# Operands laid out by numpy before the launch in a one-core hybrid decoder step: kept conv rows, cached keys, taps and sinks turned, states and second weights in whole rows

## The chip, the cores and the metric

The kernel runs on one core of a Trainium2 chip. The time is what the device takes for one execution, in microseconds; several runs are made and their median is taken. What numpy does ahead of the launch and behind it is outside this time.

## The reference

A trunk of two layers works on one prompt of 1024 tokens and on 8 decode rows of 4 tokens each (32 sample tokens), all 1024 wide. Each layer computes `x + gate * Branch(RMSNorm(x) * (1 + scale) + shift)`, and a last RMSNorm follows.

```python
# layer 0: attention, 16 heads of 64 over 4 key heads, window 128, a sink for each head;
# sample tokens also look at 128 cached keys and values of their row
k_all = jnp.concatenate([k_buf, k], axis=1)
p = sink_softmax(einsum('bqkgd,bskd->bkgqs', q, k_all) * SWA_SCALE, mask, sinks)
# layer 1: gated DeltaNet
xqkv, z, a, b = jnp.split(h @ w_in, [4096, 6144, 6160], axis=-1)
xpad = jnp.concatenate([conv_buf, xqkv], axis=1)   # 3 kept rows, then the new ones
conv = silu(depthwise_conv(xpad, conv_w))          # 4 taps on each of 4096 channels
...
o, s_new = gated_delta_chunked(q, k, v, g, beta, s0, chunk)
return o @ w_out, xpad[:, -3:], s_new
```

What the change touches are these inputs and outputs. In: `cache_swa_k` (8 rows x 128 positions x 4 heads x 64), `state_gdn_conv` (8 x 3 x 4096), `state_gdn_s` (8 rows x 16 heads x 128 x 128), `swa_sinks` (16), `gdn_conv_w` (4 x 4096) and `gdn_w_in` (1024 x 6176). Out: the last three conv inputs of the prompt and of each sample row, and the new 128 x 128 states of the prompt (16) and of the sample rows (8 x 16).

## The kernel before

**Layout.** Prompt and samples are one matrix of T = 1056 columns (TP = 1024 for the prompt, TS = 32 for the samples), cut into three column groups of 384, 384 and 288; the samples are the end of the third. A float32 product is made of three matmuls on split halves: high times high, high times low, low times high (`wh`, `wl` for weights, `hhi`, `hlo` and `h2hi`, `h2lo` for activations). A projection of one block of 128 output channels takes, for each group, 8 slices of the contraction by three matmuls; `projector` (L575 to L612) runs a list of such blocks and loads the raw weights two blocks ahead (`load_raw`, L441), which ScalarE rounds to `wh` and GpSimd subtracts to `wl` (`split_w`, L449).

**Stages**, in the times of the profiled execution: 0 to 107 us norm, modulation and the first projections; to 407 attention with its projections; to 560 its output projection and the second modulation; to 1410 the DeltaNet projections, with the conv, the triangular solves and the chain of states woven in; then the last output projection, with the sample rows' states read, updated and written, and the last norm.

**What sets the order.** Up to L1287 the instructions go to the tile framework's own scheduler, with some pinned behind others. From there on class `Core` (L96 to L175) keeps a modelled clock for each engine, and each instruction is kept in program order on its engine; every instruction passes through the helper at L89, so most rows of the profile carry that line. The kernel's parts are generators ("jobs") started by `weave` with a rank from the tables `K` and `KR` (L241, L242). Between projection matmuls the planner advances jobs whose condition holds: `ready` (operands written by now on the modelled clock), `soon` (a little later), `idle` (an engine free about now), or `bank` (one of PSUM's eight tiles free: two `pj` for projections, one `tr`, two `mi`, one `ob`, two `lg`; L232). The tables are the same in both kernels.

**The places that the change touches.**

- Sinks. `hsel`, a constant 128 x 128 selector (L59 to L63), is loaded at L1223 to L1225; 16 sinks are loaded as a column (L1248), and a matmul (L1250) spreads them to 128 partitions, from where VectorE writes them negated to `ssk` (L1251). `ssk` is used in the softmax of the cached pairs.
- Cached keys. `cached_pair` (L1067 to L1133) runs four times, each for two decode rows. It loads keys and values (`kc`, `vc`: position on the partition, 256 channels in a row), and for each row transposes four heads on TensorE (L1083) into one `mi` bank, which ScalarE copies to `KT` (L1085). Logits, softmax, two transposes of the probabilities and the value matmuls follow. `cached` (L1034 to L1063) starts the pairs once the prompt's attention is done, and behind the last pair it frees their tiles, loads the rest of the output weights and calls `begin_out`, which loads the gate's selector rows `selt`.
- Taps. `first_weights` (L1431 to L1445) loads the taps as rows (`cwr`), transposes them on TensorE into an `lg` bank, and VectorE copies them to `cw`; it also loads the first key weights `kwr`.
- Second weights. `gin` (L1313) is `gdn_w_in` seen as 128 partitions x 8 slices x 6176 columns. A raw half block is 128 partitions by 4 slices by 128 columns, so 4 pieces of 512 B for each partition. The decay columns `wab` (L1523) are pieces of 32 columns.
- Conv. `conv` (L1668 to L1730) is called for 32 blocks of 128 channels, at the projection of each. ScalarE's evacuation `evac` writes the projection to one of two tiles `XR` (channels on the partition, 3 + T columns), applies the first tap, and VectorE the others. At the third group the kept rows of the samples are loaded (`st`, 24 rows of 128 channels, L1695), and `samples()` (L1699 to L1726) waits for a `tr` bank, transposes `st` and the last 35 columns of `XR` (3 of the prompt, 32 of the samples) on TensorE, and ScalarE copies the first to `XS` and the second to `cvo`. SP then stores `cvo` in four pieces: the prompt's rows and three for the samples. GpSimd copies the samples' new columns into `XS` and does their four taps; ScalarE applies SiLU and SP stores the result. `open_["st"]` keeps the next block's third group from being evacuated before this job has ended.
- States. `states_times` (L2381 to L2421) loads the sample rows' states in tiles of four heads (`S0`, L2364), and `new_states` (L2631 to L2675) loads them again, updates them and stores them to `S1` (L2365). Each partition's share of a tile is four pieces of 512 B. The prompt's new states are stored two heads at a time (L2104).

Of the kernel before, what the change touches and what calls it, by code (L numbers as in the profile page):

```python
# [5 lines left out]
F32 = mybir.dt.float32  # L6
# [8 lines left out]
P = 128  # L15
D = 1024
KD = D // P
TP = 1024
NB = TP // P
DB = 8  # L20
# [11 lines left out]
def constants():  # L32

    i = np.arange(P)
    blocks = {}
    blocks["ident"] = np.eye(P)
    blocks["iu"] = (i[:, None] <= i[None, :]) * 1.0
    blocks["ones"] = np.ones((P, P))
    blocks["mku"] = np.where(i[:, None] <= i[None, :], 0.0, NEG)
    dist = P + i[:, None] - np.arange(2 * P)[None, :]  # L40
    blocks["wmask"] = np.where((dist >= 0) & (dist <= P), 0.0, NEG)

    t, par = i % DS, i // 16 % 2
# [15 lines left out]
    hsel = np.zeros((P, P))  # L59
    for kv in range(4):  # L60
        for r in range(32):
            hsel[kv * 4 + (r % 16) // 4, 32 * kv + r] = 1.0
    blocks["hsel"] = hsel  # L63
# [4 lines left out]
    order = ["ident", "iu", "ones", "mku", "lo32", "bsel", "fold32", "fold64", "wmask", "hsel", "smask", "selp", "sels"]  # L68
# [151 lines left out]
def body(tc, I, O, cst_ap, dbg=None):  # L220
# [299 lines left out]
    def ready(*ts):  # L520
        return lambda: plain() or nc.ready(ts) <= nc.free["tensor"]
# [4 lines left out]
    def idle(eng, *ts):  # L526
        return lambda: plain() or max(nc.free[eng], nc.ready(ts)) <= nc.free["tensor"] + AI
# [16 lines left out]
    def give(tag, t):  # L544
        q = held[tag]
        q[q.index(t.tensor.name)] = None
# [215 lines left out]
    if True:  # L762
# [304 lines left out]
        def cached_pair(b2, smk, osv):  # L1067

            kc_rows = I["cache_swa_k"][0].rearrange("b s h d -> b s (h d)")
# [3 lines left out]
            kc = sa.tile([P, 2, 256], F32, tag="kc", name="kc", bufs=2)  # L1073
            vc = sa.tile([P, 2, 256], F32, tag="vc", name="vc", bufs=2)
            nc.sync.dma_start(kc, kc_rows[bs].rearrange("b s c -> s b c"))
            nc.sync.dma_start(vc, vc_rows[bs].rearrange("b s c -> s b c"))
            KT = sa.tile([64, 2, 4, P], F32, tag="KT", name="KT", bufs=2)
            for r in range(2):
                yield ready(kc)
                pt = yield from bank("mi")  # L1080
                for kv in range(4):
# [165 lines left out]
        skc = sm.tile([16, 1], F32, tag="skc", name="skc")  # L1247
        nc.sync.dma_start(skc, I["swa_sinks"].rearrange("o h -> h o"))  # L1248
        pt = psb()
        nc.tensor.matmul(pt[:, 0:1], hsel[0:16, :], skc, start=True, stop=True)  # L1250
        nc.vector.tensor_scalar_mul(ssk, pt[:, 0:1], -1.0)  # L1251
# [240 lines left out]
    sconv = I["state_gdn_conv"][0].rearrange("b t c -> (b t) c")  # L1492
# [20 lines left out]
    def decays():  # L1513
# [128 lines left out]
    ncp = O["new_conv_p"][0, 0]  # L1642
    ncs = O["new_conv_s"][0].rearrange("b t c -> t b c")

# [7 lines left out]
    w_raw, w_split, projected = projector([(gin, [(0, c0, P)]) for c0 in plan])  # L1652
# [3 lines left out]
    if True:  # L1656
# [4 lines left out]
        open_ = {"vT": 0, "st": 0}  # L1661
# [6 lines left out]
        def conv(ct, sm0, dst, done, run=None):  # L1668
# [3 lines left out]
            cs = slice(ct * P, (ct + 1) * P)  # L1672
# [3 lines left out]
            def evac(gi, a0, b0, pj):  # L1676
                e = min(b0, TP)
                until(lambda: (n_ < 2 or convs[n_ - 2] == 4) and open_["vT"] < VB and (gi < 2 or open_["st"] == 0))
# [15 lines left out]
                if gi == 2:  # L1694
                    st = gj.tile([24, P], F32, tag="st", name="st")  # L1695
                    nc.sync.dma_start(st, sconv[:, cs])
                    open_["st"] += 1

                    def samples():  # L1699
                        yield ready(st, XR[:, TP:])  # L1700
                        pt = yield from bank("tr")
                        XS = gj.tile([P, DB, 7], F32, tag="XS", name="XS", bufs=2)
                        nc.tensor.transpose(pt[:, 0:24], st, ident[0:24, 0:24])
                        nc.tensor.transpose(pt[0:35, P:2 * P], XR[:, TP:TP + 35], ident)
                        yield soon(pt)
# [20 lines left out]
                        open_["st"] -= 1  # L1726
# [266 lines left out]
        def chain(hq, st):  # L1993
# [110 lines left out]
            nc.sync.dma_start(O["new_s_p"][0, 0, 2 * hq:2 * hq + 2].rearrange("h k d -> k h d"), S)  # L2104
# [52 lines left out]
        def run_k(evac):  # L2157
            for gi in range(2):
                until(lambda: len(opened) <= 1 - gi)
                project(gin, None, P, h2hi, h2lo, evac, kw, (gi,))  # L2160
            evacs.append(evac)
# [3 lines left out]
        proj_kq(0, states[0], (1,), lambda evac: projected(evac, lambda: project(gin, None, P, h2hi, h2lo, evacs[0], kw, (2,))))  # L2165
# [198 lines left out]
        S0 = I["state_gdn_s"][0].rearrange("b h k d -> b k h d")  # L2364
        S1 = O["new_s_s"][0].rearrange("b h k d -> b k h d")  # L2365
# [315 lines left out]
    for b in range(LB + 1):  # L2681
        out_block(b)
        if b == NB:
# [14 lines left out]
_INS = ["x_prompt", "x_sample", "cache_swa_k", "cache_swa_v", "state_gdn_conv", "state_gdn_s", "c_prompt", "c_sample",  # L2698
        "norm_g", "w_mod", "b_mod", "swa_w_in", "swa_sinks", "swa_w_out", "gdn_w_in", "gdn_conv_w", "gdn_a_log",
        "gdn_dt_bias", "gdn_o_norm_g", "gdn_w_out", "final_norm_g"]  # L2700
_OUTS = [("y_p", (1, 1024, 1024)), ("y_s", (8, 4, 1024)),
         ("new_k_p", (1, 1, 128, 4, 64)), ("new_v_p", (1, 1, 128, 4, 64)),
         ("new_k_s", (1, 8, 128, 4, 64)), ("new_v_s", (1, 8, 128, 4, 64)),
         ("new_conv_p", (1, 1, 3, 4096)), ("new_s_p", (1, 1, 16, 128, 128)),
         ("new_conv_s", (1, 8, 3, 4096)), ("new_s_s", (1, 8, 16, 128, 128))]
# [20 lines left out]
```

## Time and profile before

| what | value |
|---|---|
| median of 3 runs | 1694.86 us (1690.61 to 1696.72) |
| span of the profiled execution | 1699.2 us |
| instructions in it | 31431 |
| bytes moved | 191.76 MB, 281571 packets, 253881 of them under 2 KB |
| HBM read, written | 144.68 MB, 47.04 MB |

The profiled execution is one of its own: its span, 1699.2 us, stands beside the runs' times of 1690.61, 1694.86 and 1696.72. PE is TensorE's matmul queue and PEld its weight loads, DVE is VectorE, ACT ScalarE, POOL GpSimd, SP the queue that issues DMAs. A row of the timeline has the start in us, the duration in us, the engine, the line of the kernel, the operation, what it writes and reads, and in square brackets the idle time before it and what ended that. Matmuls are pipelined, so the duration of one is longer than the distance to the next; the distance between starts is what one costs in a full queue. A row of a list of waits has the engine and its instruction, who released it, and then the total, the number of times and the longest.

### The profile page before, as it was taken

How to read it: one execution, taken by the hardware profiler on the slowest of the kernel's cores; microseconds unless marked ns; L12 is line 12 of the kernel's file. 1: busy time of each engine (PE TensorE's matmuls, PEld its weight loads, DVE VectorE, ACT ScalarE, POOL GpSimd, SP SyncE). 2: the span in 40 equal slices, each digit the busy share in tenths (PEclk: the TensorE clock that was granted, in tenths of full speed). 3: DMA queues.
4: the chain of work that ended last, by engine and by line, in shares of the span. 5: the costliest groups of instructions: out<-in, count | busy, mean ns of one | idle time of the engine just before them, and what ended most of it. 6: DMA issues, size and time to landing. Idle time of an engine off the chain costs nothing. (4 is left out here: it accounts for less than half of the span.)

```text
span 1699.2 us, 31431 instructions
## 1 busy us (share of the span) xinstructions
PE 1613.3 (95%) x10554; PEld 1417.4 (83%) x10554; DVE 1207.9 (71%) x3540; ACT 865.5 (51%) x2517; POOL 581.8 (34%) x1042
## 2 busy tenths in 40 slices
PE   6999999998999999999999999999999998989896
PEld 4988888986678899988989999899999996667784
DVE  5526676564665578878889788788788876367776
ACT  6625565443344565366463755655656654233332
POOL 2501111111222334363442644345344454333232
PEclk9999999998999999999999999999999999999998
DMA  9532121223343232132422324124241237855885
GB/s 345 158 123 73 53 59 48 59 81 93 116 136 105 79 77 65 59 99 73 118 56 69 89 66 129 46 79 111 54 124 49 55 97 225 245 165 169 243 259 166
DMA packets 281571, 191.76 MB, mean 113 GB/s; under 512 B 98361, under 2 KB 253881, under 8 KB 281378
## 3 DMA queue, kind: packets, MB, share of 16 engines
q1 hardware_dynamic: 281410, 189.75, 38.8%
q8 instruction: 84, 1.38, 0.4%
q14 instruction: 77, 0.63, 0.1%
HBM read 144.68 MB, written 47.04 MB: 113 GB/s over the span
## 5 line engine op out<-in xcount | busy, mean ns | idle before, releaser
L89 PE MATMUL ps_pj<-h2hi,wh 128*128 128x384 f32 (+1 forms) x1128 | 380.1, 337 | 0.0
L89 PE MATMUL ps_pj<-h2hi,wl 128*128 128x384 f32 (+1 forms) x1128 | 378.9, 336 | 0.6 <-POOL wl L89 0.5
L89 PE MATMUL ps_pj<-h2lo,wh 128*128 128x384 f32 (+1 forms) x1128 | 379.3, 336 | 0.0
L89 POOL TENSOR_TENSOR wl<-wr,wh 128x512 fp32r<-128x512 f32 x122 | 165.0, 1354 | 533.2 <-ACT wh L89 470.7
L89 PEld LDWEIGHTS ps_pj<-h2hi,wl 128*128 128x128 f32 x1128 | 213.5, 189 | 4.6 <-POOL wl L89 1.2
L89 PEld LDWEIGHTS ps_pj<-h2hi,wh 128*128 128x128 f32 x1128 | 213.5, 189 | 2.4
L89 PEld LDWEIGHTS ps_pj<-h2lo,wh 128*128 128x128 f32 x1128 | 213.2, 189 | 2.6
L89 POOL TENSOR_TENSOR xt<-xt,y 128x512 f32<-128x512 f32 (+1 forms) x48 | 63.6, 1329 | 174.3 <-DVE y L89 140.7
L89 PE MATMUL ps_pj<-hlo,wh 128*128 128x384 f32 (+1 forms) x360 | 119.6, 332 | 0.0
L89 PE MATMUL ps_pj<-hhi,wh 128*128 128x384 f32 (+1 forms) x360 | 119.0, 331 | 0.0
L89 PE MATMUL ps_pj<-hhi,wl 128*128 128x384 f32 (+1 forms) x360 | 118.7, 330 | 0.0
L89 DVE SCALAR_TENSOR_TENSOR vT<-XR,cT,vT 128x384 f32<-128x384 f32 (+1 forms) x144 | 91.8, 644 | 21.8 <-ACT vT L89 20.3
L89 DVE TENSOR_TENSOR X<-X,tmp 64x31 f32<-64x31 f32 (+15 forms) x248 | 94.5, 381 | 8.5
L89 DVE TENSOR_TENSOR tmp<-X 64x31 f32<-64x31 f32 (+15 forms) x248 | 95.9, 387 | 4.8 <-POOL X L89 1.5
L89 ACT CAST wh<-wr 128x512 fp32r<-128x512 f32 x122 | 75.1, 616 | 15.3 <-PE ps_pj L89 11.9
L89 PEld LDWEIGHTS ps_pj<-hlo,wh 128*128 128x128 f32 x360 | 68.2, 189 | 11.2 <-issue 11.1
L89 ACT COPY XR<-ps_pj 128x384 f32<-128x384 f32 (+1 forms) x96 | 43.2, 450 | 64.7 <-PE ps_pj L89 64.6
L89 PEld LDWEIGHTS ps_pj<-hhi,wh 128*128 128x128 f32 x360 | 68.3, 190 | 2.7 <-issue 2.7
L89 PEld LDWEIGHTS ps_pj<-hhi,wl 128*128 128x128 f32 x360 | 68.2, 189 | 2.1 <-issue 2.1
L89 ACT ACTIVATE prob<-prob,nm 128x256 f32<-128x256 f32 (+1 forms) x128 | 62.2, 489 | 14.9 <-DVE nm L89 14.7
L89 POOL TENSOR_TENSOR Xd<-Xc,cst 32x128 f32<-32x128 f32 x128 | 63.6, 497 | 16.1 <-DVE UZ L89 6.7
L89 ACT ACTIVATE qe<-ps_mi,Eg 128x128 f32<-128x128 f32 x112 | 35.0, 364 | 65.6 <-PE ps_mi L89 65.6
(575 smaller groups left out, 4177.2 us busy)
## 6 DMA issues: line engine op xcount, KB each, us to landing
wr<-in_gdn_w_in SPq DMA_DIRECT2D x96, 256.0 KB
S<-in_state_gdn_s SPq DMA_DIRECT2D x40, 256.0 KB
xt<-in_x_prompt SPq DMA_DIRECT2D x16, 512.0 KB
wm<-in_w_mod SPq DMA_DIRECT2D x16, 512.0 KB
wr<-in_swa_w_in SPq DMA_DIRECT2D x64, 128.0 KB
wmod<-in_w_mod SPq DMA_DIRECT2D x32, 256.0 KB
wm<-in_w_mod SPq DMA_DIRECT2D x32, 256.0 KB
DP<-gcr SPq DMA_DIRECT2D x64, 128.0 KB
```

What stands on the lines that cost most here:

```text
L89: inst = fn(*args, **kwargs)
```

## The change

Before the launch `relaid()` makes new arrays from six inputs with numpy, and these are the kernel's inputs in place of the six. `conv7` (32 x 128 x 56) holds for each channel the 8 rows' three kept inputs with room for four new ones; `keysT` (4 x 64 x 1024) the cached keys with the head's channel first; `sinks_r` (128 x 1) the sinks, each repeated; `taps` (128 x 128) the taps with the channel first; `gwb` (48 blocks x 128 x 8 x 128) and `gwab` (128 x 8 x 32) the DeltaNet weights, so that one partition's share of a block is one row; `states` (8 x 128 x 16 x 128) the states with the key channel first. Three outputs have other shapes and are turned back by numpy: `new_conv` (32 x 128 x 35), `new_s_p` (128 x 16 x 128) and `new_s_s` (8 x 128 x 16 x 128).

In the kernel the transposes of cached keys, kept conv rows, last conv inputs and taps are gone, with their copies, and so are the selector matmul and its constant. The tiles `KT`, `XS`, `cT` and `ssk` are loaded directly; `ssk` is then negated in place on VectorE. The last 35 columns of `XR` are stored directly by one DMA for each block. `samples()` waits for GpSimd to be idle where it waited for a `tr` bank, and the gate `open_["st"]` is gone.

```diff
@@ cached_pair
-            kc_rows = I["cache_swa_k"][0].rearrange("b s h d -> b s (h d)")
             yield lambda: paired[0] >= b2 - 1
             bs = slice(2 * b2, 2 * b2 + 2)
-            kc = sa.tile([P, 2, 256], F32, tag="kc", name="kc", bufs=2)
             vc = sa.tile([P, 2, 256], F32, tag="vc", name="vc", bufs=2)
-            nc.sync.dma_start(kc, kc_rows[bs].rearrange("b s c -> s b c"))
+            KT = sa.tile([64, 2, 4, P], F32, tag="KT", name="KT", bufs=2)
+            nc.sync.dma_start(KT.rearrange("p r h s -> p (r h s)"), I["keysT"][b2])
             nc.sync.dma_start(vc, vc_rows[bs].rearrange("b s c -> s b c"))
-            KT = sa.tile([64, 2, 4, P], F32, tag="KT", name="KT", bufs=2)
-            for r in range(2):
-                yield ready(kc)
-                pt = yield from bank("mi")
-                for kv in range(4):
-                    nc.tensor.transpose(pt[0:64, kv * P:(kv + 1) * P], kc[:, r, kv * 64:(kv + 1) * 64], ident)
-                yield idle("scalar", pt)
-                nc.scalar.copy(KT[:, r], pt[0:64].rearrange("p (h s) -> p h s", s=P))
-                give("mi", pt)
             yield ready(KT)
@@ sinks
-        hsel = wp.tile([P, P], F32, tag="wr", name="hsel", bufs=4)
-        o, w = COFF["hsel"]
-        nc.sync.dma_start(hsel, cst_ap[:, o:o + w])
...
         ssk = sm.tile([P, 1], F32, tag="ssk", name="ssk")
-        skc = sm.tile([16, 1], F32, tag="skc", name="skc")
-        nc.sync.dma_start(skc, I["swa_sinks"].rearrange("o h -> h o"))
-        pt = psb()
-        nc.tensor.matmul(pt[:, 0:1], hsel[0:16, :], skc, start=True, stop=True)
-        nc.vector.tensor_scalar_mul(ssk, pt[:, 0:1], -1.0)
+        nc.sync.dma_start(ssk, I["sinks_r"])
+        nc.vector.tensor_scalar_mul(ssk, ssk, -1.0)
@@ first_weights
-            cwr = wp.tile([P, 512], F32, tag="wr", name="cwr", bufs=4)[:, 0:P]
-            nc.sync.dma_start(cwr, I["gdn_conv_w"].rearrange("o t (n c) -> (o t n) c", c=P))
-            kwr.extend(load_raw([(0, HQ * P, P)], gin[:, 4 * q:4 * q + 4, :], P) for q in range(2))
-            yield ready(cwr)
-            pt = yield from bank("lg")
-            nc.tensor.transpose(pt[:, 0:P], cwr, ident)
-            yield soon(pt)
-            nc.vector.tensor_copy(cw, pt[:, 0:P].rearrange("p (t n) -> p t n", n=32))
-            give("lg", pt)
+            nc.sync.dma_start(cT.rearrange("p k c -> p (k c)")[:, 0:P], I["taps"])
+            kwr.extend(load_raw([(0, 0, P)], gin[HQ][:, 4 * q:4 * q + 4, :], P) for q in range(2))
@@ conv
-                until(lambda: (n_ < 2 or convs[n_ - 2] == 4) and open_["vT"] < VB and (gi < 2 or open_["st"] == 0))
+                until(lambda: (n_ < 2 or convs[n_ - 2] == 4) and open_["vT"] < VB)
...
-                    st = gj.tile([24, P], F32, tag="st", name="st")
-                    nc.sync.dma_start(st, sconv[:, cs])
-                    open_["st"] += 1
+                    XS = gj.tile([P, DB, 7], F32, tag="XS", name="XS", bufs=2)
+                    nc.sync.dma_start(XS.rearrange("p b t -> p (b t)"), I["conv7"][ct])
 
                     def samples():
-                        yield ready(st, XR[:, TP:])
-                        pt = yield from bank("tr")
-                        XS = gj.tile([P, DB, 7], F32, tag="XS", name="XS", bufs=2)
-                        nc.tensor.transpose(pt[:, 0:24], st, ident[0:24, 0:24])
-                        nc.tensor.transpose(pt[0:35, P:2 * P], XR[:, TP:TP + 35], ident)
-                        yield soon(pt)
-                        nc.scalar.copy(XS[:, :, 0:3], pt[:, 0:24].rearrange("p (b t) -> p b t", t=3))
-                        cvo = gj.tile([35, P], F32, tag="cvo", name="cvo")
-                        nc.scalar.copy(cvo, pt[0:35, P:2 * P])
-                        give("tr", pt)
+                        yield ready(XS, XR[:, TP:])
+                        nc.sync.dma_start(O["new_conv"][ct], XR[:, TP:TP + 35])
+                        yield idle("gpsimd")
                         nc.gpsimd.tensor_copy(XS[:, :, 3:7], XR[:, 3 + TP:3 + T].rearrange("p (b t) -> p b t", t=DS))
-                        nc.sync.dma_start(ncp[:, cs], cvo[0:3])
-                        for t in range(1, DS):
-                            nc.sync.dma_start(ncs[t - 1, :, cs], cvo[3 + t:35:DS])
...
-                        open_["st"] -= 1
@@ whole rows
-        gin = I["gdn_w_in"][0].rearrange("(k p) c -> p k c", p=P)
+        gin = I["gwb"]
...
-            nc.sync.dma_start(raw, gin[:, 4 * q:4 * q + 4, 6144:6176])
+            nc.sync.dma_start(raw, I["gwab"][:, 4 * q:4 * q + 4, :])
...
-    w_raw, w_split, projected = projector([(gin, [(0, c0, P)]) for c0 in plan])
+    w_raw, w_split, projected = projector([(gin[c0 // P], [(0, 0, P)]) for c0 in plan])
...
-            nc.sync.dma_start(O["new_s_p"][0, 0, 2 * hq:2 * hq + 2].rearrange("h k d -> k h d"), S)
+            nc.sync.dma_start(O["new_s_p"][:, 2 * hq:2 * hq + 2], S)
...
-        S0 = I["state_gdn_s"][0].rearrange("b h k d -> b k h d")
-        S1 = O["new_s_s"][0].rearrange("b h k d -> b k h d")
+        S0 = I["states"]
+        S1 = O["new_s_s"]
```

More of the change, by code (lines that the diff above doesn't have):

```diff
@@ L67, in constants @@
     blocks["fold32"] = (i[:, None] % 32 == np.arange(32)[None, :]) * 1.0
-    order = ["ident", "iu", "ones", "mku", "lo32", "bsel", "fold32", "fold64", "wmask", "hsel", "smask", "selp", "sels"]
+    order = ["ident", "iu", "ones", "mku", "lo32", "bsel", "fold32", "fold64", "wmask", "smask", "selp", "sels"]
     blocks = {k: blocks[k] for k in order}
@@ L2159, in run_k @@
                 until(lambda: len(opened) <= 1 - gi)
-                project(gin, None, P, h2hi, h2lo, evac, kw, (gi,))
+                project(None, None, P, h2hi, h2lo, evac, kw, (gi,))
             evacs.append(evac)
@@ L2164, in body @@
         w_raw(1)
-        proj_kq(0, states[0], (1,), lambda evac: projected(evac, lambda: project(gin, None, P, h2hi, h2lo, evacs[0], kw, (2,))))
+        proj_kq(0, states[0], (1,), lambda evac: projected(evac, lambda: project(None, None, P, h2hi, h2lo, evacs[0], kw, (2,))))
         for r in range(HQ):
@@ L2695, in body, with relaid @@
     es.close()
-_INS = ["x_prompt", "x_sample", "cache_swa_k", "cache_swa_v", "state_gdn_conv", "state_gdn_s", "c_prompt", "c_sample",
-        "norm_g", "w_mod", "b_mod", "swa_w_in", "swa_sinks", "swa_w_out", "gdn_w_in", "gdn_conv_w", "gdn_a_log",
+_INS = ["x_prompt", "x_sample", "cache_swa_k", "cache_swa_v", "c_prompt", "c_sample",
+        "norm_g", "w_mod", "b_mod", "swa_w_in", "swa_sinks", "swa_w_out", "gdn_a_log",
         "gdn_dt_bias", "gdn_o_norm_g", "gdn_w_out", "final_norm_g"]
+def relaid(inputs):
+    A = {k: np.asarray(inputs[k]) for k in ("state_gdn_conv", "cache_swa_k", "swa_sinks", "gdn_conv_w", "gdn_w_in", "state_gdn_s")}
+    conv7 = np.zeros((32, P, DB, 7), np.float32)
+    conv7[:, :, :, 0:3] = A["state_gdn_conv"][0].reshape(DB, 3, 32, P).transpose(2, 3, 0, 1)
+    gw = A["gdn_w_in"][0].reshape(KD, P, -1).transpose(1, 0, 2)
+    more = dict(conv7=conv7.reshape(32, P, 56),
+                keysT=A["cache_swa_k"][0].reshape(4, 2, P, 4, 64).transpose(0, 4, 1, 3, 2).reshape(4, 64, 1024),
+                sinks_r=np.repeat(np.stack([A["swa_sinks"][0].reshape(4, 4)] * 2, axis=1).reshape(32), 4).reshape(P, 1),
+                taps=A["gdn_conv_w"].reshape(P, P).T, gwab=gw[:, :, 6144:6176],
+                gwb=gw[:, :, 0:6144].reshape(P, KD, 48, P).transpose(2, 0, 1, 3),
+                states=A["state_gdn_s"][0].transpose(0, 2, 1, 3))
+    return {k: np.ascontiguousarray(v, dtype=np.float32) for k, v in more.items()}
 _OUTS = [("y_p", (1, 1024, 1024)), ("y_s", (8, 4, 1024)),
@@ L2713 @@
     arrays, I, O = {}, {}, {}
[L2714 to L2715 removed]
+    laid = relaid(inputs)
+    for name in _INS + sorted(laid):
+        a = laid[name] if name in laid else np.ascontiguousarray(inputs[name])
         arrays["in_" + name] = a
@@ L2724 @@
     r = run_bass_kernel_spmd(nc, [arrays], core_ids=[0])
-    return tuple(r.results[0]["out_" + name] for name, _ in _OUTS)
+    out = [r.results[0]["out_" + name] for name, _ in _OUTS]
+    conv, s_p, s_s = out[6].reshape(32 * P, 35), out[7].transpose(1, 0, 2), out[8].transpose(0, 2, 1, 3)
+    conv_s = conv[:, 3:35].reshape(32 * P, DB, DS)[:, :, 1:DS].transpose(1, 2, 0)
+    return tuple(np.ascontiguousarray(a) for a in (*out[0:6], conv[:, 0:3].T[None, None], s_p[None, None], conv_s[None], s_s[None]))
```

17 lines of the change are left out of this document (3 added, 14 removed).

## The prediction, on record before the result

> **What bounds the kernel now.** I read the page first, then the busy time of each engine by stage, then TensorE's own waits, then the timeline of TensorE around the code that the change touches.
>
> ```profile
> span 1699.2 us, 31431 instructions
> ...
> PE 1613.3 (95%) x10554; PEld 1417.4 (83%) x10554; DVE 1207.9 (71%) x3540; ACT 865.5 (51%) x2517; POOL 581.8 (34%) x1042
> ```
>
> ```profile
> 107.00:407.00 300.00, 293.49 (x2121) 255.62 (x2121) 186.66 (x684) 157.25 (x511) 42.79 (x36) 0.99 0.26 70
> 407.00:560.00 153.00, 145.44 (x754) 112.73 (x751) 90.25 (x264) 62.53 (x143) 35.99 (x31) 0.98 0.36 111
> 560.00:1410.00 850.00, 826.33 (x5833) 778.80 (x5833) 699.66 (x1944) 492.24 (x1521) 373.44 (x825) 1.00 0.31 81
> 1410.00:1500.00 90.00, 81.58 (x467) 56.15 (x467) 36.37 (x98) 31.77 (x95) 30.64 (x71) 0.96 0.82 238
> 1500.00:1700.00 200.00, 176.08 (x781) 137.67 (x779) 147.83 (x443) 65.81 (x143) 62.52 (x46) 0.95 0.65 198
> ```
>
> The second fence has, by stretch: its length, then busy time and count of TensorE's matmuls, its weight loads, VectorE, ScalarE and GpSimd, then the granted clock, the DMA share and GB/s. TensorE is busy 95% of the span and nearly 98% of the attention projections (107 to 407) and 97% of the DeltaNet projections (560 to 1410). In those stretches the kernel is a queue of TensorE instructions, so an instruction taken out of that queue shortens the span. TensorE's holes lie between 407 and 560 and after 1410, and only after 1410 is the DMA share high beside them.
>
> **The change, part by part.**
>
> *Sample conv.* Per channel block (32 of them) two TensorE transposes and two ScalarE copies go. Their price is read as the distance between the projection matmuls on either side. I show a cheap place and a dear one.
>
> ```profile
> 568.11 0.29 PE L89 MATMUL ps_pj<-h2hi,wl 128*128 128x288 f32 x1
> 568.33 0.24 PE L89 MATMUL ps_tr<-cst,st 24*128 24x24 f32 x1
> 568.49 0.30 PE L89 MATMUL ps_tr<-cst,XR 128*35 128x128 f32 x1
> 568.55 0.38 PE L89 MATMUL ps_pj<-h2hi,wh 128*128 128x288 f32 x1
> 568.77 0.29 PE L89 MATMUL ps_pj<-h2lo,wh 128*128 128x288 f32 x1
> 568.90 0.29 PE L89 MATMUL ps_pj<-h2hi,wl 128*128 128x288 f32 x1
> ```
>
> ```profile
> 901.68 0.53 PE L89 MATMUL ps_pj<-h2hi,wh 128*128 128x384 f32 x1
> ...
> 902.35 0.42 PE L89 MATMUL ps_pj<-h2lo,wh 128*128 128x384 f32 x1
> 902.61 0.34 PE L89 MATMUL ps_pj<-h2hi,wl 128*128 128x384 f32 x1
> 902.79 0.38 PE L89 MATMUL ps_mi<-S,qT 128*128 128x256 f32 x1
> ```
>
> In the first, two steps take 568.11 to 568.77 = 0.66 us where two undisturbed ones take 0.13 each (568.77 to 568.90): 0.40 us lost. In the second, 901.68 to 902.61 = 0.93 where undisturbed ones take 0.18 each (902.61 to 902.79): 0.57. I take the middle, 0.48, so 32 x 0.48 = **15.4 us** (12.8 to 18.2). ScalarE's two copies lie beside TensorE and count nothing themselves. In their place SP issues one load and one store per block where it issued one load and four stores, so SP is held less. The new load fills the tile that GpSimd reads; its slot was last read two blocks earlier, and the planner opens the evacuation only when that block's sample part is done, so no queue stands behind it. The store reads the evacuated tile itself, whose next writer also comes two blocks later.
>
> *Cached keys.* 32 transposes and 8 ScalarE copies go.
>
> ```profile
> 381.93 0.30 PE L89 MATMUL ps_pj<-hhi,wl 128*128 128x288 f32 x1
> 382.11 0.60 PE L89 MATMUL ps_mi<-cst,kc 128*64 128x128 f32 x4
> 382.46 0.38 PE L89 MATMUL ps_pj<-hhi,wh 128*128 128x288 f32 x1
> ```
>
> ```profile
> PE ps_mi L89 <- DMA kc<-in_cache_swa_k: 1.4, 1, 1.4
> ```
>
> The second fence is TensorE's wait for the first keys: total, times, longest. Four transposes put 0.53 us between projections that stand 0.13 apart: 0.40, eight times = **3.2 us** (2.4 to 4). The 1.4 us that TensorE waited for the first keys is not counted as a gain: in the changed order the logits of the first two pairs stand where the first transposes stood, behind a load issued at the same place. Nor is ScalarE's share of the wait before the first softmax, which the changed order keeps.
>
> *The end of the cached pairs* is where a wait goes. Columns as before; the number in brackets is idle time.
>
> ```profile
> 407.24 0.29 PE L89 MATMUL ps_pj<-hhi,wl 128*128 128x288 f32 x1
> ...
> 409.74 0.41 PE L89 MATMUL ps_mi<-cst,sp 128*128 128x128 f32 x2 [0.65 <-DVE sp L89]
> 410.96 0.30 PE L89 MATMUL ps_ob<-spT,vss 128*64 128x32 f32 x2 [0.81 <-DVE spT L89]
> ...
> 414.56 3.75 PE L89 MATMUL ps_lg<-modG,selt 128*128 128x512 f32 x4 [2.58 <-issue]
> ```
>
> The projections, the only cover, run out at 407.24 with two pairs unfinished. In the changed order the third pair's value matmuls stand 14 projections before the end and the last pair's transposes one before it. Past the last projection only the copy of the last pair (409.74 to 410.96 = 1.2), its value matmuls (0.9) and then the load of the gate's selector rows (2.6) are late: 4.7 us where there were 7.3. That is **2.6 us** (0, if the softmax is late again, to 4.5).
>
> *Sinks and taps.* The rows are one of the selector matmul's, then SP, VectorE and TensorE near 40 us.
>
> ```profile
> L1250 PE MATMUL ps_mi<-skc,hsel x2: 245/256/266, 107.0 to 107.1; 16*128 16x1 f32 x2
> 39.98 0.42 SPq L1248 DMA_DIRECT2D skc<-in_swa_sinks  x1
> 41.85 2.61 DVE L675 TENSOR_TENSOR hlo<-fu,hhi 128x1024 fp32r<-128x1024 f32 x1 [0.72 <-ACT hhi L674]
> 46.18 0.34 PE L702 MATMUL ps_pj<-hlo,wh 128*128 128x384 f32 x1
> ```
>
> The selector matmul (two passes of 0.25 us) and one transpose, by its row no dearer, go: **0.6 us** (0 to 0.8). But a wait is added. The negation of the sinks now stands on VectorE ahead of the subtraction that began at 41.85, and waits for a load issued at 39.98. Behind it stands that subtraction, due on TensorE at 46.18. It ended at 44.46, so 1.7 us of lateness is hidden, and I count nothing (0 to 2 lost). The load of the taps waits for the last modulation matmul, as the weight buffers behind it did already: nothing.
>
> *Whole rows* (weights, states in and out, new states): the bytes stay, the 512 B pieces become rows of 2 or 4 KB.
>
> ```profile
> 0.00:50.00 50.00, 33.40 (x199) 22.75 (x200) 27.73 (x80) 29.88 (x45) 17.20 (x21) 1.00 0.94 316
> 1600.00:1650.00 50.00, 49.63 (x229) 40.63 (x228) 38.62 (x131) 16.43 (x38) 15.69 (x12) 1.00 0.83 251
> ```
>
> ```profile
> PE ps_lg L89 <- DMA S<-in_state_gdn_s: 2.3, 3, 1.9
> PE ps_mi L89 <- ACT kb L89: 6.6, 4, 3.4
> PE ps_tr L89 <- ACT vT L89: 7.2, 5, 2.5
> ```
>
> ```profile
> 1583.91 0.62 ACT L89 CAST ohi<-of 128x512 fp32r<-128x512 f32 x1 [2.68 <-DMA of<-gTd]
> ```
>
> The start loads mostly long rows and moves 316/0.94 = 336 GB/s per full share; 1600 to 1650 moves mostly states, 251/0.83 = 302. So a byte in long rows costs about a tenth less. Before 1410 the share is 0.26 to 0.36 and the weights come a projection ahead, so it buys nothing there. After 1410 it shortens the queue. Three waits for states are worth 2.3 us. The longest wait for the state update's scaled keys (3.4 of the 6.6) ended just after 1585 and came from ScalarE standing 2.68 us behind a load of gated rows that shared the queue. I take the 2.3 and half of the 3.4: **4.0 us**; the ends are 0 (the queue empties no sooner) and 10 (all of 2.3 and 6.6, and 1 of clock). The new pieces of 140 and 224 B are 64 small transfers in 850 us at a DMA share of 0.31: nothing.
>
> A rule that speaks against this term: the Trainium skill, "DMA: Bandwidth & Descriptors", section Specifications, puts the line rate at transfers of 512 B and more, so that rows beyond 512 B would win nothing and only the added short rows would change. By it the sum would be 4.0 smaller. The two rows above (336 against 302) speak mildly against it.
>
> *The sum*: 15.4 + 3.2 + 2.6 + 0.6 + 4.0 = 25.8 us. The profiled execution has a span of 1699.2, so it would become 1673.4. That execution is 4.3 us longer than the median of the runs (1694.86), and I carry the difference over: 1694.86 - 25.8 = **1669.1 us**, 1.5% less.
>
> The rest of the order is reassuring. From the 161st matmul of the last output projection on it is the same in both kernels, so what the planner rearranges lies between about 380 and 1490.
>
> **The rivals.** A measurement of this kernel tells about 0.5% (8.5 us) from no change.
>
> ```profile
> 391.00:396.00 5.00, 3.71 (x14) 3.73 (x15) 3.53 (x11) 1.14 (x5) 1.04 (x3) 0.67 0.16 47
> ```
>
> 1. *Half is given back.* The planner's constants stay while the work changes, so a consumer can now follow its producer too closely. A wait also lowers the clock: a hole of 1.9 us just before 392.3 left 0.67 of the clock over 391 to 396. Five waits like the longest for the value tile (2.5 us) cost 12.5: 1694.9 - 25.8 + 12.5 = 1682. For it: 23.7 us of holes in 850 show a close fit. Against it: fewer users of the one bank that transposes share. The Trainium skill, "TensorE: Matmul & The Clock Gate", section on the HAM clock gate, lets the clock fall after an idle window of about 3.4 us; in this trace 1.9 us did it.
> 2. *Nothing visible.* The transposes filled holes that stay as waits, and the pieces do not matter: 1693. Against it: matmuls stand back to back on both sides in the first two timelines.
> 3. *More.* The end of the kernel loses its DMA waits and the slow clock behind them: 10 instead of 4.0, and 3 of the transposes' upper bound: 1660.
> 4. *Slower.* One mechanism: between 560 and 1410 the rearranged sample part and the freed bank let value transposes be issued before ScalarE has made their tile (7.2 us in five waits today). It must cost 25.8 + 8.5 = 34 us to show as slower, 14 waits of 2.5; the stretch's holes would grow from 23.7 to 58. At 40 us it gives 1709.
> 5. *The long rows buy nothing.* If 512 B pieces already move at the full rate, the queue after 1410 stays as long and its 4.0 us fall: 1694.9 - 21.8 = 1673, inside the forecast's own range. The two rows of 336 and 302 GB/s speak against it, mildly, since stores are in the second. This is what the rule of the Trainium skill named above would give.
>
> **How the numbers follow.** The forecast has 0.47 and rival 5, which the same range holds, 0.15; half back 0.20, more 0.08, nothing 0.05, slower 0.05. The bounds of the terms alone give 1694.9 - 37.5 = 1657 to 1694.9 - 13.2 = 1682. The range runs from 1657 to 1685, which takes in the forecast, most of rivals 1 and 3, and leaves out nothing and slower. Faster by over 0.5%: 0.47 + 0.15 + 0.08 + 0.18 = 0.88; within: 0.02 + 0.05 = 0.07; slower: 0.05.
>
> **What would show it.** The count of TensorE matmuls falls by 99, and 560 to 1410 gets some 15 us shorter with about 24 us of holes; if these holes are 35 or more, rival 1 holds. Between the last attention projection and the selector matmul lie about 5 us, not 7.3. After 1410 the waits for states are gone and the granted clock over 1500 to 1700 rises above 0.95; if they stay, the 4.0 falls. TensorE late at 46.18 would show the sinks' wait. The prediction is wrong altogether if TensorE's holes grow with the instructions that it loses.

## The result: 1.7% slower

The changed kernel takes 1723.94 us in the median of 4 runs (1722.56 to 1725.51), the kernel before 1695.79 beside it. The ratio is 1.017, with a 95% interval of 1.015 to 1.0191. The forecast was 1669.1, in a range of 1657 to 1685. The direction was wrong, and the time lies beyond the fourth rival's 1709.

The head of the page of the changed kernel:

```profile
span 1723.7 us, 31005 instructions
## 1 busy us (share of the span) xinstructions
PE 1613.6 (94%) x10455; PEld 1419.3 (82%) x10455; DVE 1211.7 (70%) x3539; ACT 850.4 (49%) x2445; POOL 594.6 (34%) x1042
```

The 99 matmul instructions went, from 10554 to 10455 as forecast, and ScalarE issues 72 instructions less. Yet TensorE's busy time stayed (1613.3 before), and 24.5 us were added to the span.

To find where, I match the work: the projection matmuls (those that write `ps_pj`, or a bank that stands in for it) come in the same order in both kernels, so the n-th of them can be set beside the n-th. The changed kernel is 0.2 us late at 376.8, 5.5 early at 431.1 and 6.3 early at 566.4, as the conv stage begins. From there on it loses: 18.5 late at 1390.3 and 24.5 at the end. So the DeltaNet stage, between the matmul that starts at 566.4 before (560.1 after) and the one at 1390.3 (1408.9), costs 24.9 us more, and what follows 5.9 more. The busy time over that matched stage, first before, then after (columns as in the prediction: length, matmuls, weight loads, VectorE, ScalarE, GpSimd, granted clock, DMA share, GB/s):

```profile
566.40:1390.30 823.90, 800.53 (x5612) 754.82 (x5611) 683.24 (x1909) 480.85 (x1499) 360.25 (x804) 1.00 0.30 80
```

```profile
560.10:1408.90 848.80, 804.93 (x5549) 760.21 (x5548) 690.78 (x1910) 468.56 (x1434) 372.54 (x804) 0.98 0.27 78
```

TensorE's holes (length less busy time) grew from 23.4 to 43.9 us. Its busy time grew too, though the 64 transposes are missing (63 by the rows' counts): the clock was 0.98 in place of 1.00. The clock fell around the longest holes:

```profile
600.00:640.00 40.00, 32.92 (x194) 32.59 (x194) 31.17 (x86) 22.70 (x60) 18.50 (x21) 0.87 0.20 54
720.00:760.00 40.00, 32.11 (x180) 28.74 (x180) 27.91 (x84) 22.01 (x76) 17.54 (x57) 0.87 0.36 99
```

What TensorE waited for in that stage (total, times, longest):

```profile
PE ps_tr L84 <- ACT vT L84: 15.1, 13, 7.1
PE ps_tr L84 <- ACT vo L84: 4.7, 4, 2.0
PE ps_lg L84 <- POOL Xd L84: 4.6, 2, 3.8
PE ps_lg L84 <- ACT kT L84: 3.8, 1, 3.8
PE ps_mi L84 <- DVE us L84: 3.8, 5, 1.3
PE ps_ob L84 <- DVE vo L84: 2.8, 4, 1.6
```

The wait for the value tile doubled (7.2 before), but it is one of many: no single producer is late everywhere. The longest hole, followed back over four engines' timelines:

```profile
619.08 0.30 PE L84 MATMUL ps_pj<-h2hi,wl 128*128 128x288 f32 x1
626.45 0.90 PE L84 MATMUL ps_tr<-cst,vT 128*128 128x128 f32 x3 [7.08 <-ACT vT L84]
```

```profile
612.95 0.62 ACT L84 ACTIVATE vT<-XR,cT 128x384 f32<-128x384 f32 x1
618.87 0.23 ACT L84 ACTIVATE us<-us 128x32 f32<-128x32 f32 x1 [5.31 <-POOL us L84]
619.12 1.28 ACT L84 ACT_TABLE_LOAD   x1
620.41 2.19 ACT L84 ACTIVATE DP<-DP 128x512 f32<-128x512 f32 x4
622.61 1.28 ACT L84 ACT_TABLE_LOAD   x1
...
625.88 0.51 ACT L84 ACTIVATE vT<-vT 128x384 f32<-128x384 f32 x1
```

```profile
620.43 0.60 DVE L84 SCALAR_TENSOR_TENSOR vT<-XR,cT,vT 128x384 f32<-128x384 f32 x1
```

```profile
610.57 2.34 POOL L84 TENSOR_SCALAR tp<-XS,cT 128x32 f32<-128x32 f32 x1
612.99 0.34 POOL L84 TENSOR_TENSOR us<-us,tp 128x32 f32<-128x32 f32 x1
613.31 0.38 POOL L84 TENSOR_SCALAR tp<-XS,cT 128x32 f32<-128x32 f32 x1
613.78 1.49 POOL L84 TENSOR_TENSOR us<-us,tp 128x32 f32<-128x32 f32 x1
615.24 1.46 POOL L84 TENSOR_TENSOR wl<-wr,wh 128x512 fp32r<-128x512 f32 x1
```

TensorE's value transposes stood ahead of its projections and waited for ScalarE, which had idled 5.31 us in front of the samples' SiLU, because GpSimd was late with the samples' taps (one of them took 2.34 us where its like took 0.38, and a weight split stood among them). Behind the SiLU came the exponentials with two table loads, and only then the value tile. VectorE's last tap of that tile ended at 621.03, so about 2 of the 7 us would have been left without this. Every one of these instructions exists in the kernel before; their places in the queues are new.

### The profile page after: what moved, and what is told of

It reads as the page before. It is cut to its first block, busy times and chain, and to the rows that moved or that the text cites. A ratio compares the mean times of both kernels' runs of the same rounds, so it can differ in the third digit from the quotient of the medians.

```text
span 1723.7 us, 31005 instructions
## 1 busy us (share of the span) xinstructions
PE 1613.6 (94%) x10455; PEld 1419.3 (82%) x10455; DVE 1211.7 (70%) x3539; ACT 850.4 (49%) x2445; POOL 594.6 (34%) x1042
## 5 line engine op out<-in xcount | busy, mean ns | idle before, releaser
L84 DVE SCALAR_TENSOR_TENSOR vT<-XR,cT,vT 128x384 f32<-128x384 f32 (+1 forms) x144 | 88.2, 622 | 39.9 <-ACT vT L84 38.0
L84 DVE CUSTOM_DVE_ANT_0 prob<-ps_lg,cst 128x256 f32<-128x256 f32 (+1 forms) x128 | 46.9, 402 | 33.9 <-DMA out_new_v_p<-vsb 24.1
```

The costliest lines, as they stand in the source:

```text
L84: inst = fn(*args, **kwargs)
```

## The experiments

Three theories. **A**: the conv part's new order fits badly, and that is the whole loss. **C**: any new order of the DeltaNet stage is worse than the one of before, whatever causes the re-planning. **D**: the new load and store of the conv part hold SP's queue. B, that the long rows or direct loads cost the time, is the rival to all of them.

Executions of the kernel before stand beside each run: their medians are 1697.25 us for 1 to 4, 1696.63 for 5 to 8 and 1698.76 for 9 to 12. Differences in us are between medians; each ratio has its 95% interval.

**1. The conv part alone.** The edit is the diff's part on `conv`, with its input and output, made on the kernel before.

> The kernel before with the sample conv part alone: kept rows loaded laid out, last 35 columns stored directly, no transposes, the planner free to plan anew. Theory A (the planner, now without the transposes and their bank, puts instructions of the DeltaNet stage in another order that fits the engines badly; the keys, sinks, taps and rows are innocent): 1720 to 1735, with holes of TensorE over 560 to 1410 as in the changed kernel (about 45 us instead of 24). Rival B (the long rows or the direct loads at the start and the end cost the time): about 1680. Rival C (each re-plan costs some time, from whichever part): somewhat above 1696, about half of the loss.

1720.87 us, ratio 1.0137 (1.0091 to 1.0182). The conv part alone brings the loss. B falls. In the trace TensorE's matmuls stand over the matched stage in the same sequence as in the changed kernel, all 5546 of them, so the other parts of the change did not alter this order.

**2. The conv part in the old order.** The planner's clocks are charged for the removed instructions; nothing is issued for them, and the new load and store are not charged. The gate `open_["st"]` stays. Here `st` and `cvo` are names that only the planner knows. The lines are cut where `...` stands.

```diff
-                        yield ready(XS, XR[:, TP:])
...
-                        yield idle("gpsimd")
+                        yield ready(st, XR[:, TP:])
+                        pt = yield from bank("tr")
+                        nc.issued("tensor", "transpose", None, (pt[:, 0:24], st, ident[0:24, 0:24]), {})
+                        nc.issued("tensor", "transpose", None, (pt[0:35, P:2 * P], XR[:, TP:TP + 35], ident), {})
+                        yield soon(pt)
+                        nc.issued("scalar", "copy", None, (XS[:, :, 0:3], pt[:, 0:24]), {})
...
+                        nc.issued("scalar", "copy", None, (cvo, pt[0:35, P:2 * P]), {})
+                        give("tr", pt)
```

> The conv part alone again, but the planner's modelled clocks and bank are charged for the removed transposes, copies and transfers as if they were still there, so that TensorE, VectorE, ScalarE and GpSimd keep the order of the kernel before with the removed instructions left out. Only the queue of transfers on SP differs. Theory A: the priced gain appears, 1695.8 - 15.4 = about 1680 (1677 to 1684). Rival D (the new load and store hold SP's queue while they wait for GpSimd's taps and for ScalarE's evacuation, and the transfers behind them come late): the loss stays, 1700 to 1725 as in the changed kernel.

1689.21 us, ratio 0.9955 (0.9938 to 0.9972). The same work removed, the same new transfers, but the old order: 0.45% faster in place of 1.4% slower. So the loss is the order of the queues, SP's among them, not the work: between 1 and 2 lie 31.7 us. TensorE's sequence over the matched stage is that of the kernel before without its 64 transposes. The time lies between A's 1677 to 1684 and D's 1700 to 1725: the gain is only 8.0 us where 15.4 were priced.

**3. Everything but the conv part.** The changed kernel with the conv's lines of before.

> The changed kernel with its sample conv part put back as before (transposes, copies, four stores); keys, sinks, taps, weights and states stay laid out by numpy. Theory A: the gain of 3.2 + 2.6 + 0.6 + 4.0 appears, 1685 to 1690. Rival B: 1710 or more, since the cause would be in these parts. Rival C: 1695 to 1715, the gain lost to an order planned anew from the attention stage on.

1691.86 us, ratio 0.9971 (0.9951 to 0.9991): 5.4 us less than before, just outside A's 1685 to 1690 and far from B's 1710. Although the attention stage was planned anew, the order of the DeltaNet stage is again that of before, but for 13 of 5610 matmuls, and the stage is 824.5 us long, as before.

**4 and 8. The kernel before with the planner nudged.** One constant of the modelled clock, by 0.005 us; the work is complete and the same.

```diff
-0.06 if op == "copy" and srcs[0].space == PSUM
+0.065 if op == "copy" and srcs[0].space == PSUM
...
-0.13 if op == "scalar_tensor_tensor" else 0.08
+0.135 if op == "scalar_tensor_tensor" else 0.08
```

> The kernel before, all work kept, with one constant of the planner's modelled clock changed by 0.005 us (the fixed cost of a ScalarE copy from PSUM, 0.060 to 0.065). The instructions are the same, their order is planned anew from the attention stage on. Rival C (the tables fit only the one order that they were set for, so any new plan is slower): 1705 to 1725, with more holes over 560 to 1410. Theory A in its narrow form (only the conv part's own change of the order hurts), and rivals B and D: 1696, within 5 us.

> The kernel before with another constant of the planner moved by 0.005 us (the fixed cost of VectorE's three-operand operations, 0.130 to 0.135). Theory C: 1705 to 1725 again. If the first nudge was bad luck: 1690 to 1700.

1715.41 (ratio 1.0109, 1.0073 to 1.0144) and 1714.89 (1.0117, 1.0095 to 1.0139). A nudge that removes and adds nothing costs 18 us. Theory A in its narrow form falls: it isn't only the conv part that fits badly, it is any order of the DeltaNet stage but the old one, as far as tried.

**7. The changed kernel nudged**, by the first of these constants.

> The changed kernel with the planner's constant moved by 0.005 us as in the nudged kernel before. If any order but the one that the tables were set for costs about 15 to 30 us (theory C), 1700 to 1730, on either side of the changed kernel's 1724. If the changed kernel's loss is a lasting property of the conv part's new work (theory A in its narrow form), 1720 to 1728 again.

1719.57, ratio 1.0149 (1.0127 to 1.0171). Another order, but one near the changed kernel's (about 600 of the 5546 matmuls stand elsewhere), and about the same loss; 0.4 us below the second range, it tells little between the two.

**5 and 6. The whole change in the old order, and with SP's queue mended.** The first is the edit of 2 on the changed kernel. The second also gives two places on SP's queue (the arguments of the dependences are shortened):

```diff
+                    if stored:
+                        tc.add_manual_dep(ld.ins, stored[-1].ins.name, NoSync)
...
+                        stored.append(nc.sync.dma_start(smd[sm0], uf))
+                        out = nc.nc.sync.dma_start(O["new_conv"][ct], XR[:, TP:TP + 35])
+                        tc.add_manual_dep(out.ins, stored[-1].ins.name, NoSync)
```

> The whole change, with the planner's clocks and bank charged for the sample conv's removed work as before. Its order on TensorE, ScalarE, VectorE and GpSimd is that of the kernel before, without the removed instructions, except for the attention stage and its end. If the loss of the changed kernel is the new order alone (theory A and C), the two gains measured so far add up: 8.0 for the conv part and 5.4 for the rest below the kernel before, about 1683 (1679 to 1687). If the two parts disturb each other, 1690 or more.

> The same as the run before it, but on SP's queue each load of the kept rows stands behind the store of the block before it, and each store of the last 35 columns behind the store of its own block's samples, so that neither is at the head of the queue before its tile is free or written. The engines' orders are the same. Rival D (the missing half of the priced 15.4 us is transfers held up behind these two): 5 to 7 us less than the run before it, and SP no longer waits for GpSimd's taps or for XR. If the missing half is other engines that TensorE now waits for: no change, within 2 us.

1689.48 (ratio 0.9966, 0.9947 to 0.9984) and 1686.30 (0.9944, 0.9924 to 0.9963). Both beat both kernels, and the first misses its 1679 to 1687. What SP's queue waited for over 560 to 1410, in the first, then in the second:

```profile
SPq L1688 <- ACT XR L84: 61.9, 17, 13.5
SPq L1672 <- POOL us L84: 53.4, 20, 6.9
```

```profile
SPq L84 <- ACT us L84: 67.3, 21, 7.8
SPq L84 <- POOL XS L84: 58.9, 10, 14.0
SPq L84 <- POOL tp L84: 40.3, 5, 16.9
```

The two named waits are gone and others came. The 3.2 us between the medians lie between D's 5 to 7 and the 2 that would count as no change. The matched DeltaNet stage is not shorter (816.9 and 820.3 us); with the clock taken out the two are alike (last table). What follows the stage takes 311.5 us in the first and 306.0 in the second, in one order on the four engines, at a granted clock of 0.95 and 0.97. So D does not show where it should; whether the mended queue gains anything stays open.

The first is 7.2 us under the kernel before, where 2 and 3 sum to 13.4. Its DeltaNet stage is 7.0 shorter, but what follows the stage takes 311.5 us, against 308.9 before, 303.7 in 2 and 306.9 in 3, all in the same order. Single executions differ by this much: run 9, whose attention stage is that of before, begins the DeltaNet stage 5.9 us early. So whether the two gains add up is not shown.

**9. Whole rows alone**, and **10. cached keys alone**, each on the kernel before; the diff's lines for them.

> The kernel before with whole rows alone: second weights, states in and new states out as rows of 2 to 4 KB; nothing else changed, the same order on all engines. By the prediction's term 4.0 us less than before, about 1692.5, with the end of the kernel (after 1410) shorter. By the prediction's rival 5 (the rows buy nothing): 1696, within 1.5 us.

> The kernel before with the cached keys alone laid out, planned anew; the order is new in the attention stage's end and the same from the output projection on. By the prediction's terms 3.2 + 2.6 = 5.8 us less than before, about 1691, seen between the last attention projections and the output projection. If the end of the cached pairs was luck of the order: 3.2 us or less, 1693.5 or more.

Rows: 1703.33, ratio 1.0016 (1.0001 to 1.003), so nothing gained and perhaps 0.2 to 5 us lost. Keys: 1693.54, ratio 0.9967 (0.9951 to 0.9983), 5.2 us less (2.9 to 8.3 by the interval) where 5.8 were priced; in absolute time it touches the other branch's 1693.5, but the kernel before was at 1698.76 beside it. The rows did make the transfers cheaper: 202979 packets in place of 281571. The last 280 us of before and 284 of the rows run:

```profile
1410.00:1690.00 280.00, 257.66 (x1247) 193.82 (x1246) 180.13 (x525) 96.13 (x235) 92.45 (x117) 0.96 0.72 215
```

```profile
1406.00:1690.00 284.00, 256.21 (x1212) 192.23 (x1210) 180.03 (x521) 96.09 (x236) 92.15 (x116) 0.96 0.67 211
```

The share fell from 0.72 to 0.67 at about the same GB/s (299 and 315 per full share). But the waits stayed, in the rows run:

```profile
PE ps_mi L89 <- ACT kb L89: 7.5, 3, 4.6
PE ps_lg L89 <- DMA S<-in_states: 3.1, 3, 2.3
```

They were 6.6 and 2.3 before: with cheaper transfers these waits did not get shorter.

**11. Each of the 64 sample transposes twice**, on the kernel before and in its order; the second ones compute nothing that is used.

> The kernel before with each of the 64 transposes of the sample conv issued twice, the second ones into an unused part of the same bank and not charged to the planner, so that the order is that of before. It asks what one such pair costs the kernel. By the prediction's price (0.48 us a pair, TensorE alone sets the pace): 15 us more, about 1711. If TensorE shares the pace with other engines, as the conv part in the old order suggests (8.0 us for 32 pairs): 8 us more, about 1704.

1710.18, ratio 1.0057 (1.0038 to 1.0077): 11.4 us more (6.5 to 13.1 by the interval), which takes in the 8 and leaves out the 15. The matched stage, here and then with the pairs removed in the old order (experiment 2):

```profile
562.30:1399.40 837.10, 813.83 (x5676) 764.67 (x5675) 681.18 (x1909) 481.77 (x1499) 357.69 (x804) 0.99 0.30 79
```

```profile
565.40:1383.40 818.00, 789.16 (x5548) 749.15 (x5547) 683.77 (x1908) 470.83 (x1435) 364.79 (x804) 1.00 0.31 81
```

Added, 32 pairs make TensorE 13.3 us busier and the holes stay at 23.3: the stage is 13.2 longer. Removed, they take 11.4 us of busy time away, but the holes grow from 23.4 to 28.8, and the stage is only 5.9 shorter. Part of this difference is the clock: it stood at half for 13.7 us of the stage with the pairs doubled, for 6.8 before and in 2. The last table takes this out.

**12. The samples' SiLU later**, in the changed kernel:

```diff
-                        yield soon(uf)
+                        yield lambda: nc.ready((uf,)) + 4.0 <= nc.free["tensor"]
```

> The changed kernel, planned so that ScalarE's SiLU of the samples is issued only when GpSimd's taps have been done for 4 us by the planner's clock. In the changed kernel ScalarE waited 32.4 us for these taps over 560 to 1410 (17.5 before), and the two longest holes of TensorE (7.2 and 4.0 us) follow such waits. Theory E (this one placement is the loss): ScalarE's wait falls below 15 us and the time to 1700 or less. Theory C (any new order is about 15 to 30 us worse than the one that the tables were set for): the wait falls, other waits take its place, 1710 to 1730.

1720.59, ratio 1.0117 (1.0095 to 1.0138). ScalarE's wait for the taps is gone from the list of waits, where it was 32.4 us in the changed kernel, and other waits stand in its place:

```profile
ACT vT L84 <- DVE vT L84: 28.5, 19, 4.5
ACT qT L84 <- DVE qT L84: 20.5, 12, 3.5
```

So taking away the placement behind the longest holes (7.1 and 3.8 us by the rows above) does not help. As the whole order is new again, this shows no more than that.

**All kernels side by side.** The table has the matched DeltaNet stage. There the granted clock of the traces stands at full or at half, at half for 3.4 us or a multiple of it (before, 580.4 to 583.8). Holes are its length less TensorE's busy time, and the last column is an estimate: the length less half of the time at half clock.

| kernel | order of the stage | length, us | holes, us | at half clock, us | length at full clock, us |
|---|---|---|---|---|---|
| before | old | 823.9 | 23.4 | 6.8 | 820.5 |
| 3, all but conv | old | 824.5 | 24.5 | 3.4 | 822.8 |
| 9, rows alone | old | 822.3 | 23.8 | 3.4 | 820.6 |
| 10, keys alone | old | 828.1 | 26.6 | 10.2 | 823.0 |
| 11, transposes twice | old | 837.1 | 23.3 | 13.7 | 830.3 |
| 2, conv part | old | 818.0 | 28.8 | 6.8 | 814.6 |
| 5, whole change | old | 816.9 | 25.3 | 10.2 | 811.8 |
| 6, SP's queue mended | old | 820.3 | 25.2 | 17.1 | 811.8 |
| 4, nudged before | new | 840.0 | 34.7 | 13.7 | 833.2 |
| 8, nudged before | new | 838.5 | 35.8 | 13.7 | 831.7 |
| 1, conv part | new | 847.3 | 48.6 | 23.9 | 835.4 |
| changed kernel | new | 848.8 | 43.9 | 37.5 | 830.0 |
| 7, nudged after | new | 842.8 | 43.7 | 23.9 | 830.9 |
| 12, late SiLU | new | 844.0 | 42.7 | 20.5 | 833.8 |

Every old order has 23 to 29 us of holes, every new one 35 to 49. The order decides. At full clock the old order takes 820.5 to 823.0 with the 64 transposes and 811.8 to 814.6 without them, about 9 us less, and the doubled ones cost about 9 more: a pair is worth some 0.28 us either way. A new order takes 830 to 835, with the transposes or without.

## Why the prediction was wrong

- *"In those stretches the kernel is a queue of TensorE instructions, so an instruction taken out of that queue shortens the span."* It holds only while the queue keeps its order. The planner made another one, and that cost more than the instructions: 31.7 us between 1 and 2, which issue the same work, and 34.5 between the changed kernel and 5. This is the step that failed, and with it the sentence that called the rest of the order reassuring because "what the planner rearranges lies between about 380 and 1490": in that stretch lies the DeltaNet stage, where the old order left TensorE 23.4 us of holes and the new one 43.9. The sum had no term for the rearranging; it stood only in the first rival (12.5 us, chance 0.20) and the fourth (34 us, 0.05).
- *The order isn't all.* In the old order the whole change takes 1689.48 and at best 1686.30 us, still above the range's 1685: terms of the sum were too large as well, the conv's and the rows' above all.
- *The cost of the new order*, read from the matched stage against experiment 2's: 11.4 us of work went, 20.5 us of holes came, and the remaining work took 804.9 at a clock of 0.98 where it took 789.2 at 1.00, so 15.7 more. That makes 24.8 of the 24.9 us; it divides the loss and proves no cause. The time at half clock (37.5 us against 6.8) accounts for 15.4 of the 15.7 by estimate. Run 1 has the same order in this stage with 48.6 us of holes and 23.9 at half clock, so the division changes from one execution to another.
- *The sign of being wrong* that the prediction named came: TensorE's holes grew with the instructions that it lost, beyond the 35 us set for the first rival too.
- *Sample conv, 15.4 us.* In the old order 8.0 by the medians, about 9 by the table. The price of 0.48 a pair was too high for two reasons. The middle of a cheap and a dear place is not the mean: in the trace of before the same distance takes 0.66 to 0.80 us at 19 of the 32 places and 0.94 or more at six. This place, at 0.75 (1303.43 to 1304.18) with undisturbed steps of 0.18, is common, and it gives 0.39:

```profile
1303.43 0.34 PE L89 MATMUL ps_pj<-h2lo,wh 128*128 128x384 f32 x1
1303.69 0.24 PE L89 MATMUL ps_tr<-cst,st 24*128 24x24 f32 x1
1303.86 0.30 PE L89 MATMUL ps_tr<-cst,XR 128*35 128x128 f32 x1
1303.92 0.42 PE L89 MATMUL ps_pj<-h2hi,wl 128*128 128x384 f32 x1
1304.18 0.34 PE L89 MATMUL ps_pj<-h2hi,wh 128*128 128x384 f32 x1
1304.36 0.34 PE L89 MATMUL ps_pj<-h2lo,wh 128*128 128x384 f32 x1
```

And of TensorE's busy time, some 0.35 a pair, a part came back as holes (25.2 to 28.8 us in 2, 5 and 6, where 23.4 to 26.6 stand with the transposes), which the price of an instruction in a full queue doesn't show.
- *SP is held less.* It isn't, by the trace: the load of the kept rows and the store of the last columns stand at the head of SP's queue and wait for GpSimd's taps and for the evacuation, as the first fence of experiments 5 and 6 shows. In the changed kernel these waits are 48.1 and 57.9 us over 560 to 1410, and all of SP's waits there sum to 627 us where they were 543 before. By experiment 6 this decided nothing that could be seen in the stage.
- *Cached keys and their end, 3.2 + 2.6.* Right: 5.2 us (2.9 to 8.3 by the interval). In the changed kernel the last projection matmul starts at 405.45 and the selector's at 409.72, 4.3 us apart as against 7.3 before (about 5 forecast).
- *Sinks and taps, 0.6, with 0 to 2 lost at the wait.* The wait was there, in the middle of its bounds:

```profile
44.27 0.15 DVE L1230 TENSOR_SCALAR ssk<-ssk 128x1 f32<-128x1 f32 x1 [3.00 <-DMA ssk<-in_sinks_r]
44.34 3.36 DVE L670 TENSOR_TENSOR hlo<-fu,hhi 128x1024 fp32r<-128x1024 f32 x1
```

```profile
47.75 0.44 PE L697 MATMUL ps_pj<-hlo,wh 128*128 128x384 f32 x1 [1.29 <-DVE hlo L670]
```

- *Whole rows, 4.0.* Nothing, as rival 5 had it. The waits that I read as the queue's length did not shorten with cheaper transfers, and the sign named for it failed: in the changed kernel the waits for states are 5.2 us where they were 2.3, and the clock over the last 200 us is 0.95, as before. The rule of the Trainium skill ("DMA: Bandwidth & Descriptors", section Specifications), which I set aside, names the same result; its reason isn't borne out in full, since the share of the DMA engines did fall (0.72 to 0.67).
- *The rivals.* The first and the fourth named the right place, and even this mechanism (a consumer that follows its producer too closely, and the clock behind the hole). Their price was wrong: the fourth asked for 34 us from the value tile alone, while its wait rose by 8 and the rest came from all the other waits and from the clock.

What stays open: whether another setting of the planner's tables would give the changed kernel an order as good as the old one, and why the old order is better than the five new ones (1 and the changed kernel have one between them). No run searched for an order.

## What to carry to other kernels

Where a planner writes out the order of a full stage, price a change twice: the instructions that go, in the old order, and the new order, about which the profile of before says nothing. A nudge of a planner's constant by 0.005 us, with the work unchanged, gives a first idea of the second; here it is 18 us, more than the change won in the old order. For the change itself the order cost 31.7 and 34.5 us, so a nudge alone would have priced it too low. If the planner is charged for the removed work as if it were there, the order stays and the gain appears, here 10.3 us (ratio 0.9944) in the best version.

## What the hardware did that I had not expected

GpSimd's small operation on 128x32 elements took 2.34 us at 610.57 and 0.38 at 613.31; the samples' seven operations took 7.7 us in that block, 2.2 to 2.9 in most others (profile spans on GpSimd are rough). VectorE was busy without a break around 610, and some of its own operations were slow there too: one on 64x60 elements took 1.20 us at 608.10 where its like on 64x87 took 0.24 at 612.71. That the two engines held each other up was not tried.
